# A gated delta rule inside a transformer trunk: queries and values turned by VectorE and DRAM instead of TensorE, log-gate sums spread by a repeating DMA read

## The chip, the cores and the metric

The kernel runs on one core of one Trainium2 chip. The metric is the device time of one launch in microseconds (us); the number compared is the median of several runs. A core has five engines that run their own instruction streams: TensorE (PE in the profile; its weight loads are listed apart as PEld), VectorE (DVE), ScalarE (ACT), GpSimd (POOL) and SyncE (SP), which in this kernel issues the DMAs. They meet by semaphores. Memory on the core is SBUF and the accumulators of TensorE, PSUM; DRAM is outside and reached by DMA.

## The reference

A trunk of two layers over a sequence of 1024 tokens with 1024 features, all in float32. Layer 0 mixes tokens by a gated spatial MLP beside a gated delta rule, layer 1 by differential attention; each layer then has an MLP and a gated projection. The change touches the delta rule of layer 0 only:

```python
def gated_deltanet(qkv, z, beta_logit, a_logit, conv_w, a_log, dt_bias, out_gain):
    qkv = silu(causal_depthwise_conv(qkv, conv_w))     # 4 taps
    q, k, v = split(qkv)                               # 4 heads of 128
    q = l2_normalize(q) * 128 ** -0.5
    k = l2_normalize(k)
    beta = sigmoid(beta_logit)
    g = -exp(a_log) * softplus(a_logit + dt_bias)      # log gates
    o = chunk_gated_delta_rule(q, k, v, g, beta)
    return rms_norm(o, out_gain) * silu(z)

def chunk_gated_delta_rule(q, k, v, g, beta):          # per chunk and head
    gc = cumsum(g)
    diff = gc[:, None] - gc[None, :]
    decay = where(causal, exp(diff), 0)
    a = where(strict, (k * beta) @ k.T * decay, 0)
    u = solve(a + I, v * beta)                         # unit lower triangular
    w = solve(a + I, k * beta * exp(gc)[:, None])
    qk = q @ k.T * decay
    # then, chunk after chunk, with a state S (128 x 128 per head):
    v_new = u - w @ S
    o = (q * exp(gc)[:, None]) @ S + qk @ v_new
    S = S * exp(gc[-1]) + (k * exp(gc[-1] - gc)[:, None]).T @ v_new
```

## The kernel before, in words

All large products are float32, made as three products of a high and a low part (`mm3`, L206), so most of TensorE's time goes to them, and ScalarE and VectorE split the operands into the parts (`split`, L222 to L224).

Activations lie with features on partitions and tokens along the free axis. The projection to queries, keys and values (`proj_qkv`) makes, per half of the sequence (512 tokens) and per 128 features, a PSUM tile of 128 x 512; VectorE adds the normalization's row factor, runs the four taps of the convolution, ScalarE a tanh, and VectorE finishes the silu into the home tile `qkv[i, hf]` (i is 0 for queries, 1 for keys, 2 for values; hf the half).

The delta rule works in 8 chunks (NC) of 128 tokens, 4 heads (G) each. It comes in four stages:

- `gates()`: TensorE makes the sums of log gates within each chunk, `gsum`, tokens on partitions, one column for each chunk and head.
- `ahead(c)`: for a chunk, the factors exp(gc_i - gc_j) as two masked tiles, `am` (strict) and `du` (causal, the other way round). One of the two sums must run along the free axis and be the same on all partitions; TensorE makes that spread: `pd` is gsum's column, broadcast, times an identity, in a high and a low part (`gparts`, `identr`). ScalarE takes the exponentials (L1602), GpSimd cuts the triangle (L1603). The keys are turned to tokens on partitions by TensorE (`pk`), normalized, and multiplied with themselves (`pkk`); VectorE puts the product and the mask together (L1628). Results go to DRAM (`spill`, and the diagonal blocks to `diag`).
- `solve()`: VectorE inverts the 32 x 32 diagonal blocks of all chunks at once, between filler work.
- the chunk loop: `inverse(c)` assembles the inverse of a chunk (`py`, `pz`), `prep(c)` turns the chunk's values and queries to tokens on partitions by TensorE transposes (`pv`, `pq`), scales the values (ScalarE), takes the queries' lengths and makes `pkq`; `step(c, state)` runs the recurrence (`pks`, `pvn`, `po`, `pst`). `prep(c + 1)` and `inverse(c + 1)` are issued beside `step(c)`.

Beside this chain of small matmuls runs a stream of filler units: the remaining projections, the spatial MLP's and the output's mm3 products, in pieces of a few large matmuls. `pump(n)` issues units up to a count; the numbers FILLA (40), FILLB (64), FILLC (48) and FILLS say how many units go beside each stage, and `share` deals them out over a stage's slots. The work of the chain is issued with priority; TensorE's own order follows the order in which the code asks for it, with a lag of 3 slots for filler. The other engines' queues are ordered by the scheduler of the framework from that program order. A PSUM buffer of the kind "aux" has two copies, shared by `pd` and `pkk`; a small pool of 4 SBUF tiles (`tmp`) serves tanh, convolution and others. SBUF tiles of fixed places (`slot`) are reused by name: "c2" and "c3" hold `du` of even and odd chunks, "c6" and "d0" hold `am`.

The last MLP of the kernel already has a turn through DRAM (L516 to L524): VectorE transposes a 128 x 512 tile in blocks of 32 x 32, and four DMAs, issued by SP, write its 32-row bands in runs of 32 numbers (128 bytes) to a DRAM tile `by_token`, so that a plain read returns the transposed tile.

## Time and profile before

| | us |
|---|---|
| median of 3 runs | 2506.88 (2506.01 to 2507.93) |
| the profiled execution | 2511.96 |
| its span | 2510.2 |
| TensorE busy | 2482.4 (99%) |
| VectorE busy | 1858.0 (74%) |
| ScalarE busy | 1288.9 (51%) |
| GpSimd busy | 315.3 (13%) |

The profile is one execution; its granted TensorE clock is 0.998 of full speed throughout. Busy is the time in which an engine worked, so a share of 99% means an engine with hardly any idle time, while an engine at 74% may still be full in one stage and idle in another. A row like "PE pkk L76 <- ACT dec L1602: 2.4, 2, 1.2" is a wait: the engine, its tile and line, then the engine and line that ended the wait, then us in total, how many times, and the longest. "x8" after a name counts instructions; a tile's name has no number where a view groups them. "landing" is the time from a DMA's issue until its data are there. Rows of a tile give the shortest, median and longest duration in ns, then the first and last start in us.

The layer-0 mixing covers the span's first 460 us: projections alone up to 95, `ahead` from 95 to about 145, `solve` to about 190, then the chunk loop.

### The profile page before, as it was taken

Reading aid. Unit: us, or ns where it says so; the run is one execution under the profiler, and the core shown is the slowest. Engines: PE = TensorE matmul, PEld = TensorE weight load, DVE = VectorE, ACT = ScalarE, POOL = GpSimd, SP = SyncE. Lnnn points to the kernel's source line nnn. Section 1 sums busy time; section 2 is a strip of 40 time slices with the busy share of each in tenths; the row PEclk is TensorE's granted clock in tenths of the full one; section 3 lists DMA queues with packets and bytes.
Section 4 is the critical chain, followed back from the end, with each engine's and each line's share of the span. In section 5 each row is a group of like instructions: output and inputs, shape, how many; then the busy total and the mean of one; then the engine's idle time right before and its main releaser. Section 6 shows DMA issues by size and latency. Waiting matters only on the chain.

```text
span 2510.2 us, 39961 instructions
## 1 busy us (share of the span) xinstructions
PE 2482.4 (99%) x13694; PEld 2117.7 (84%) x13694; DVE 1858.0 (74%) x3604; ACT 1288.9 (51%) x2585; POOL 315.3 (13%) x280
## 2 busy tenths in 40 slices
PE   9999999999999999999999999999999999999999
PEld 7898898888888887888899999987788888878877
DVE  7876767697667879566568888785886677888678
ACT  6543344465455444453356766664654445445443
POOL 0211232000000000000234443431000000000000
PEclk9999999999999999999999999999999999999999
DMA  7453435447556856653347776799475558657873
GB/s 237 128 161 84 134 111 180 145 157 239 173 195 208 271 178 196 188 172 115 118 96 170 164 170 152 168 250 279 127 229 194 178 189 275 214 189 202 232 221 109
DMA packets 530628, 451.46 MB, mean 180 GB/s; under 512 B 222484, under 2 KB 395512, under 8 KB 530424
## 3 DMA queue, kind: packets, MB, share of 16 engines
q1 hardware_dynamic: 530408, 448.90, 59.5%
q8 instruction: 108, 1.77, 0.3%
q14 instruction: 96, 0.79, 0.1%
q10 hardware_dynamic: 16, 0.00, 0.0%
HBM read 316.66 MB, written 132.12 MB: 179 GB/s over the span
## 4 chain that ended last, share of the span: by engine, by line
PE 92%; DMA 3%; DVE 3%; issue 1%; SPq 0%; ACT 0%; POOL 0%; DVEq 0%; ACTq 0%; POOLq 0%
PE mm L76 81%; PE po L76 3%; PE qk L76 3%; PE aux L76 2%; DMA raw<-in_w_ple_gate_dram 1%; PE tr L79 1%; DMA aT<-a_dram 1%; DVE w L224 0%; PE pz L76 0%; PE py L76 0%; PE aux L79 0%; PE pvn L76 0%; DMA ol<-o_dram 0%; PE pab L79 0%; PE pkq L76 0%
## 5 line engine op out<-in xcount | busy, mean ns | idle before, releaser
L76 PE MATMUL mm<-g,w 128*128 128x512 f32 x2592 | 603.8, 394 | 1.4 <-DVE acc L284 0.8
L223 ACT CAST w<-raw 128x512 fp32r<-128x512 f32 x598 | 365.6, 617 | 447.1 <-PE mm L76 348.5
L76 PEld LDWEIGHTS mm<-g,w 128*128 128x128 f32 x2592 | 485.8, 188 | 117.0 <-ACT w L223 1.2
L76 PE MATMUL mm<-hi,w 128*128 128x512 f32 x1728 | 554.3, 397 | 0.3 <-ACT hi L1268 0.3
L76 PE MATMUL mm<-w,hi 128*128 128x256 f32 (+2 forms) x2528 | 501.7, 294 | 1.3 <-ACT hi L223 1.3
L224 DVE TENSOR_TENSOR w<-raw,w 128x512 fp32r<-128x512 f32 x510 | 347.9, 690 | 169.1 <-ACT w L223 164.5
L76 PEld LDWEIGHTS mm<-w,hi 128*128 128x128 f32 x2528 | 400.8, 188 | 16.5 <-ACT hi L223 1.8
L76 PEld LDWEIGHTS mm<-hi,w 128*128 128x128 f32 x1728 | 324.9, 188 | 73.9 <-ACT hi L1268 0.7
L76 PE MATMUL mm<-w,lo 128*128 128x256 f32 (+2 forms) x1264 | 369.1, 293 | 0.8 <-DVE lo L224 0.8
L76 PE MATMUL mm<-lo,w 128*128 128x512 f32 x864 | 341.7, 396 | 0.9 <-DVE lo L1269 0.9
L76 PE MATMUL mm<-t,w 128*128 128x512 f32 x1152 | 270.8, 394 | 1.2 <-ACT w L223 1.2
L76 PEld LDWEIGHTS mm<-t,w 128*128 128x128 f32 x1152 | 216.2, 188 | 52.7 <-ACT w L223 1.6
L76 PEld LDWEIGHTS mm<-w,lo 128*128 128x128 f32 x1264 | 238.1, 188 | 7.1 <-DVE lo L224 1.2
L76 PEld LDWEIGHTS mm<-lo,w 128*128 128x128 f32 x864 | 162.8, 189 | 36.9 <-DVE lo L1269 1.4
L224 DVE TENSOR_TENSOR g<-graw,g 128x512 fp32r<-128x512 f32 x216 | 147.1, 685 | 12.7 <-DMA gd<-g 8.0
L223 ACT CAST g<-graw 128x512 fp32r<-128x512 f32 x216 | 132.7, 617 | 38.2 <-DMA graw<-gd 17.9
L260 POOL TENSOR_TENSOR r<-ms,mhalf 128x4 f32<-128x4 f32 x12 | 13.4, 1114 | 1043.0 <-DVE ms L258 1014.6
L1050 ACT ACTIVATE lg<-lg,nm 128x128 f32<-128x128 f32 (+7 forms) x128 | 99.2, 775 | 75.6 <-DVE nm L1047 74.7
L224 POOL TENSOR_TENSOR w<-raw,w 128x512 fp32r<-128x512 f32 (+1 forms) x88 | 114.9, 1325 | 145.9 <-ACT w L223 93.2
L350 ACT ACTIVATE g<-g 128x512 f32<-128x512 f32 x96 | 60.5, 631 | 116.5 <-DVE g L284 109.5
L1047 DVE CUSTOM_DVE_ANT_0 lg<-qk,al 128x512 f32<-128x512 f32 (+3 forms) x128 | 74.7, 587 | 28.9 <-PE qk L76 24.4
L76 PE MATMUL mm<-ohi,w 128*128 128x512 f32 x256 | 87.8, 408 | 0.0
(334 smaller groups left out, 3546.2 us busy)
## 6 DMA issues: line engine op xcount, KB each, us to landing
raw<-in_w_mlp_dram SPq DMA_DIRECT2D x352, 256.0 KB, 3.5
graw<-gd SPq DMA_DIRECT2D x224, 256.0 KB, 2.9
gd<-g SPq DMA_DIRECT2D x192, 256.0 KB, 3.3
raw<-in_w_ple_gate_dram SPq DMA_DIRECT2D x76, 256.0 KB, 3.3
acc<-h_dram SPq DMA_DIRECT2D x64, 256.0 KB, 4.3
keep<-in_w_mlp_dram SPq DMA_DIRECT2D x64, 256.0 KB, 4.2
raw<-in_w_in_e_dram SPq DMA_DIRECT2D x60, 256.0 KB, 3.5
h_dram<-acc SPq DMA_DIRECT2D x48, 256.0 KB, 2.6
```

The source lines that it names most:

```text
L76: self._next(self.engine.matmul(*a, **k))
L79: self._next(self.engine.transpose(*a, **k))
L223: self.nc.scalar.copy(hi, src)
L224: (lo_engine or self.nc.vector).tensor_tensor(lo, src, f32(hi), ALU.subtract)
L260: nc.gpsimd.tensor_tensor(r, ms, self.mhalf[:, 0:4], ALU.pow)
L350: nc.scalar.activation(g, src, AF.Relu)
L1047: nc.vector.tensor_tensor_reduce(out=lg[:, k0:k1], in0=ps[:, : k1 - k0], in1=al[:, u0 + k0 : u0 + k1], scale=-1.0, scalar=3.0e38 if c == 0 ...
L1050: nc.scalar.activation(lg[:, :n], lg[:, :n], AF.Exp, bias=nm[:, r, nch - 1 : nch], scale=-1.0, accum_out=me.sums[:, b, r : r + 1])
```

## The change

1. **The spread of the sums.** `ahead` loses its eight `pd` matmuls per chunk, and `gparts` and `identr` go. Instead `gates()` transposes `gsum` once on TensorE (`pgt`, 32 x 128), VectorE copies it, and SP writes it to a DRAM tile `g_dram`. `ahead(c)` begins with a DMA that reads the chunk's four rows (2 KB) into all 128 partitions of `du` (256 KB), yields, and takes both exponentials from that tile, the second in place.
2. **The interleaving of `ahead`.** A chunk's `ahead` has now three parts, and the loop over slots runs up to three chunks at once, with 10 slots for the 40 filler units instead of 9.
3. **Queries and values.** When a 128 x 512 tile of queries or values is ready, `turn()` transposes it in blocks on VectorE, and GpSimd issues four DMAs (64 KB each, runs of 128 bytes) to a DRAM tile `by_token`. There are 16 such tiles, so 16 transposes and 64 DMAs. `prep(c)` loses the TensorE transposes `pv` and `pq`; SP reads the chunk's values and queries, 256 KB each, from DRAM. ScalarE's scaling and squares then read SBUF instead of PSUM. Values have no home tile before that read.
4. **Smaller moves.** The spatial weights (`wsr`) are loaded early, into a place of their own, before the rest of the rows of x. The filler counts change: 108 units before `ahead` instead of 104, and 23 instead of 24 in each of the first four chunks. Keys are still turned by TensorE.

```diff
-FILLS = (24, 24, 24, 24, 28, 28, 28, 28)
+FILLS = (23, 23, 23, 23, 28, 28, 28, 28)
...
-        self.identr = self.cp.tile([P, P], F32R, name="identr")
-        nc.vector.tensor_copy(self.identr, self.ident)
...
         gsum, nsum = carve([P, NC, G], 0), carve([P, NC, G], 0)
-        gparts = self.cp.tile([P, 2, NC, G], F32R, name="gparts")
+        g_dram = self.dp.tile([NC * G, P], F32, name="g_dram")
...
             nc.vector.tensor_copy(flat(gsum), pg[:, 0])
-            self.split(flat(gsum), flat(gparts[:, 0]), flat(gparts[:, 1]))
+            pt = aux([NC * G, P], "aux", "pgt")
+            self.pe.transpose(pt, flat(gsum), self.ident)
+            gt = self.tmp(P)[0 : NC * G]
+            nc.vector.tensor_copy(gt, pt)
+            nc.sync.dma_start(g_dram, gt)
             nc.vector.tensor_scalar(flat(nsum), pg[:, 0], -1.0, None, ALU.mult)
-            wsr = self.tmp().rearrange("p (g t) -> p g t", g=G)
-            nc.sync.dma_start(wsr, ws.rearrange("g t s -> t g s"))
...
-        qkv, made = {}, set()
+        qkv, made, by_token = {}, set(), {}
+        def home(i, hf):
+            if (i, hf) not in qkv:
+                qkv[i, hf] = self.slot(f"A{i + 3 * hf}", [P, G, HT], F32, "qkv")
+        def turn(i, hf, m, y, t):
+            nc.vector.transpose(t, y)
+            for a in range(4):
+                f0 = m * P + 32 * a
+                nc.gpsimd.dma_start(by_token[i, hf].rearrange("(t c) f -> c t f", c=32)[:, :, f0 : f0 + 32], t[32 * a : 32 * a + 32].rearrange("c (t r) -> c t r", r=32))
+        def read_tokens(i, c, out):
+            hf, n = c // 4, c % 4
+            assert all((i, hf, m) in made for m in range(G))
+            nc.sync.dma_start(flat(out), by_token[i, hf][n * P : (n + 1) * P])
         def proj_qkv(i, j, hfs):
             def units(w):
                 for hf in hfs:
-                    if (i, hf) not in qkv:
-                        qkv[i, hf] = self.slot(f"A{i + 3 * hf}", [P, G, HT], F32, "qkv")
+                    if i != 2:
+                        home(i, hf)
+                    if i != 1 and (i, hf) not in by_token:
+                        by_token[i, hf] = self.dp.tile([4 * P, G * HD], F32, name=self.nm("by_token"))
...
                         th = self.tmp()
                         nc.scalar.activation(th, y, AF.Tanh, scale=0.5)
-                        nc.vector.scalar_tensor_tensor(qkv[i, hf][:, m % 4], th, 1.0, y, ALU.add, ALU.mult)
+                        z = y if i == 2 else qkv[i, hf][:, m % 4]
+                        nc.vector.scalar_tensor_tensor(z, th, 1.0, y, ALU.add, ALU.mult)
+                        if i != 1:
+                            turn(i, hf, m % 4, z, th)
...
         def ahead(c):
-            out = []
-            pd = aux([P, G, P], "aux", "pd")
-            for h in range(G):
-                for i in range(2):
-                    self.pe.matmul(pd[:, h], lhsT=gparts[:, i, c, h : h + 1].to_broadcast([P, P]), rhs=self.identr, start=i == 0, stop=i == 1)
-            for own, other in ((gsum, 1), (nsum, -1)):
-                e = self.slot(("c6", "d0")[c % 2] if other > 0 else f"c{2 + c % 2}", [P, G, P], F32, "dec")
+            du = self.slot(f"c{2 + c % 2}", [P, G, P], F32, "dec")
+            nc.sync.dma_start(flat(du), g_dram[G * c : G * c + G].rearrange("h t -> (h t)").partition_broadcast(P))
+            yield
+            am = self.slot(("c6", "d0")[c % 2], [P, G, P], F32, "dec")
+            for e, own, other in ((am, gsum, 1), (du, nsum, -1)):
                 for h in range(G):
-                    nc.scalar.activation(e[:, h], pd[:, h], AF.Exp, scale=-float(other), bias=own[:, c, h : h + 1])
+                    nc.scalar.activation(e[:, h], du[:, h], AF.Exp, scale=-float(other), bias=own[:, c, h : h + 1])
                 nc.gpsimd.affine_select(e, e, pattern=[[0, G], [-other, P]], base=0, channel_multiplier=other, compare_op=ALU.is_gt if other > 0 else ALU.is_ge, fill=0.0)
-                out.append(e)
-            am, du = out
             keep(c, 1, du)
...
         def prep(c):
-            k, v = part(1, c), part(2, c)
             kt = fetch(c, 2, self.slot(f"c{c % 2}", [P, G, HD], F32, "kt"))
             du = fetch(c, 1, self.slot(f"c{2 + c % 2}", [P, G, P], F32, "dec"))
-            pt = aux([P, G, P], "tr", "pv")
+            home(2, c // 4)
+            k, vb = part(1, c), flat(qkv[2, c // 4])[:, (c % 4) * HT : (c % 4 + 1) * HT].rearrange("p (h d) -> p h d", h=G)
+            read_tokens(2, c, vb)
+            if c == 0:
+                yield
+            q = part(0, c)
+            qt = self.slot(("d0", "c6")[c % 2], [P, G, HD], F32, "qt")
+            read_tokens(0, c, qt)
+            yield
             for h in range(G):
-                self.pe.transpose(pt[:, h], v[:, h], self.ident)
-            vb = v
-            for h in range(G):
-                nc.scalar.activation(vb[:, h], pt[:, h], AF.Copy, scale=hb[:, c, h : h + 1])
-            yield
-            q = part(0, c)
-            pt = aux([P, G, P], "tr", "pq")
-            for h in range(G):
-                self.pe.transpose(pt[:, h], q[:, h], self.ident)
-            rq = inverse_length(pt, "rq", self.slot(("d0", "c6")[c % 2], [P, G, HD], F32, "sq"))
+                nc.scalar.activation(vb[:, h], vb[:, h], AF.Copy, scale=hb[:, c, h : h + 1])
+            rq = inverse_length(qt, "rq", qt)
             yield
...
+        wsr = self.slot("c8", [P, G, P], F32, "wsr")
+        nc.sync.dma_start(wsr, ws.rearrange("g t s -> t g s"))
...
-        pump(104)
+        pump(108)
...
         systems = [ahead(c) for c in range(NC)]
-        for i, n in enumerate(share(FILLA, NC + 1)):
-            if i < NC:
-                run(systems[i], False)
-            if i:
-                run(systems[i - 1], False)
+        for i, n in enumerate(share(FILLA, NC + 2)):
+            for j in range(min(i, NC - 1), max(0, i - 2) - 1, -1):
+                run(systems[j], False)
             self.pe.slot()
             pump(done + n)
...
         f0 = prep(0)
-        chunk(none, invs[0], f0, FILLC, ("pi", "i", "i", "i", ""))
+        chunk(none, invs[0], f0, FILLC, ("pi", "i", "i", "i", "p"))
         chunk(none, none, f0, 0, ("p", "p"))
```

On TensorE, in the `ahead` stage before the change: the `pd` matmuls of a later chunk (`gparts` is the sums, `identr` the identity) come right ahead of the `pkk` (keys times keys) of an earlier one, and these ahead of transposes `pk`.

```order
L76 MATMUL mm_1324<-hi_201,w_1245 128x512
L76 MATMUL mm_1423<-hi_129,w_1080 128x512
L76 MATMUL mm_1423<-lo_130,w_1080 128x512
L76 MATMUL mm_1423<-hi_129,w_1081 128x512
L76 MATMUL pd_1268<-identr,gparts 128x128 x8
L76 MATMUL pkk_1310<-qkv_276 128x128 x4
L76 MATMUL mm_1423<-hi_138,w_1080 128x512
L79 MATMUL pk_1455<-ident,qkv_691 128x128 x3
L79 MATMUL pk_1526<-ident,qkv_691 128x128 x3
L76 MATMUL mm_1423<-lo_139,w_1080 128x512
```

And the same stage after the change:

```order
L76 MATMUL mm_1506<-hi_359,w_1091 128x512
L76 MATMUL mm_1506<-lo_360,w_1091 128x512
L76 MATMUL mm_1506<-hi_359,w_1092 128x512
L76 MATMUL mm_1506<-hi_405,w_1109 128x512
L76 MATMUL pkk_1414<-qkv_274 128x128 x4
L76 MATMUL pkk_1491<-qkv_274 128x128 x4
L79 MATMUL pk_1471<-ident,qkv_701 128x128
L79 MATMUL pk_1539<-ident,qkv_701 128x128
```

The `pd` rows are gone, and the `pkk` of two chunks follow each other.

GpSimd, in the `ahead` stage before: powers (`rk`), the masks (AFFINE_SELECT on `dec`, the tiles of `am` and `du`) and memsets.

```order
L1582 TENSOR_TENSOR rk_1465<-l_279_1462,mhalf 128x4
L1582 TENSOR_TENSOR rk_1536<-l_289_1533,mhalf 128x4
L1603 AFFINE_SELECT dec_1355<-dec_1355 128x512
L1603 AFFINE_SELECT dec_1361<-dec_1361 128x512
L1695 MEMSET xt_2338 128x512
L1695 MEMSET xt_2695 128x512
L1582 TENSOR_TENSOR rk_1624<-l_307_1621,mhalf 128x4
L1582 TENSOR_TENSOR rk_1695<-l_317_1692,mhalf 128x4
L1603 AFFINE_SELECT dec_1442<-dec_1442 128x512
L1603 AFFINE_SELECT dec_1448<-dec_1448 128x512
L1603 AFFINE_SELECT dec_1513<-dec_1513 128x512
L1603 AFFINE_SELECT dec_1519<-dec_1519 128x512
```

GpSimd in the same stage after, where `dec_1527`, `dec_1603` and `dec_1668` are `am` of chunks 5, 6 and 7:

```order
L1712 MEMSET xt_2326 128x512
L1379 DMA by_token_426<-t_1449 32x16x32 x4
L1623 AFFINE_SELECT dec_1527<-dec_1527 128x512
L1712 MEMSET xt_2718 128x512
L1604 TENSOR_TENSOR rk_1625<-l_306_1622,mhalf 128x4
L1623 AFFINE_SELECT dec_1457<-dec_1457 128x512
L1604 TENSOR_TENSOR rk_1690<-l_318_1687,mhalf 128x4
L1379 DMA by_token_1505<-t_1593 32x16x32 x4
L1623 AFFINE_SELECT dec_1603<-dec_1603 128x512
L1623 AFFINE_SELECT dec_1525<-dec_1525 128x512
L1379 DMA by_token_1505<-t_1734 32x16x32 x4
L1623 AFFINE_SELECT dec_1668<-dec_1668 128x512
```

Three groups of four DMAs of turned tiles stand in these rows between the masks; each waits for the VectorE transpose of its tile, and what is behind it in GpSimd's queue waits with it.

VectorE, in the `ahead` stage after: 21 rows stand between the filler weight `w_1656` (L222) and the operations that join product and mask of chunk 4 (`dec_1459` at L1646). These are the last of them, right behind the turn of a tile of values, STREAM_TRANSPOSE at L1376 (`carved` is a tile of small vectors):

```order
L222 TENSOR_TENSOR w_1836<-raw_1833,w_1835 128x512
L1636 TENSOR_SCALAR sc_1554<-rk_1549 128x4
L1639 TENSOR_TENSOR carved_240<-carved_240,rk_1549 128x4
L1420 TENSOR_SCALAR t_1588<-cx_1585,cols,t_1588 128x512
L1601 TENSOR_REDUCE l_318_1687<-sq_1685 128x4
L1632 TENSOR_TENSOR kt_1692<-pk_1680,carved_240 128x512
L1637 TENSOR_TENSOR sc_1486<-sc_1486,carved_240 128x4
L1602 TENSOR_SCALAR l_306_1622<-l_306_1622 128x4
L1637 TENSOR_TENSOR sc_1554<-sc_1554,carved_240 128x4
L1420 TENSOR_SCALAR t_1588<-cx_1585,cols,t_1588 128x512
L1602 TENSOR_SCALAR l_318_1687<-l_318_1687 128x4
L1646 TENSOR_SCALAR dec_1459<-pkk_1559,sc_1486,dec_1459 128x128 x4
```

TensorE uses that weight in the three rows ahead of the `pkk` of chunk 6, whose PSUM buffer these L1646 operations free:

```order
L76 MATMUL mm_1756<-w_1655,hi_199 128x256
L76 MATMUL mm_1756<-w_1656,hi_199 128x256
L76 MATMUL mm_1756<-w_1655,lo_200 128x256
L76 MATMUL pkk_1700<-qkv_701 128x128 x4
L76 MATMUL mm_1756<-w_1223,hi_127 128x256
```

Before the change, the rows around the same operations of VectorE (`dec_1442` and `dec_1513` are chunks 4 and 5) were these:

```order
L1404 TENSOR_SCALAR qkv_426<-t_1575,t_1570 128x512
L1628 TENSOR_SCALAR dec_1442<-pkk_1546,sc_1470,dec_1442 128x128 x4
L1395 TENSOR_TENSOR cx_1722<-mm_1579,rb_668 128x512
L1618 TENSOR_SCALAR sc_1700<-rk_1695 128x4
L1619 TENSOR_TENSOR sc_1700<-sc_1700,carved_242 128x4
L1620 TENSOR_TENSOR carved_242<-sc_1700,carved_242 128x4
L224 TENSOR_TENSOR w_1586<-raw_1583,w_1585 128x512
L1401 TENSOR_SCALAR t_1725<-cx_1722,cols,t_1725 128x512
L1628 TENSOR_SCALAR dec_1513<-pkk_1634,sc_1541,dec_1513 128x128 x4
```

Ahead of chunk 4's joining stand more rows than before: a turn, and the lengths, products and powers of the next chunks' keys (L1601, L1632, L1636, L1639).

VectorE at the start of the chunk loop, after the change (`qkv_2293` is queries; `inv_2317` the inverse of chunk 0, whose transpose TensorE's `py` waits for):

```order
L1424 TENSOR_SCALAR qkv_2293<-t_2376,t_2371 128x512
L1416 COPY carved_240<-cx_2437 128x3
L1420 TENSOR_SCALAR t_2441<-cx_2437,cols,t_2441 128x512
L1376 STREAM_TRANSPOSE t_2376<-qkv_2293 128x512
L1420 TENSOR_SCALAR t_2441<-cx_2437,cols,t_2441 128x512 x2
L1413 MEMSET cx_2539 128x3
L1758 TENSOR_SCALAR qkv_2336<-pks_2724,carved_240,qkv_2336 128x128 x4
L1424 TENSOR_SCALAR qkv_2293<-t_2446,t_2441 128x512
L1376 STREAM_TRANSPOSE t_2446<-qkv_2293 128x512
L1710 STREAM_TRANSPOSE inv_2317<-inv_2317 128x128
L1715 COPY xt_2326<-inv_2317 32x4x32 x4
```

Two turns of queries stand ahead of the transpose of `inv`; before, there were no turns on VectorE in this part.

## The prediction

> **What bounds the kernel now.** I read the busy totals first, then the chain of work that ended last, then the waits of the busiest engine in the stage that the change touches.
>
> ```profile
> span 2510.2 us, 39961 instructions
> PE 2482.4 (99%) x13694; PEld 2117.7 (84%) x13694; DVE 1858.0 (74%) x3604; ACT 1288.9 (51%) x2585; POOL 315.3 (13%) x280
> PE 92%; DMA 3%; DVE 3%; issue 1%; SPq 0%; ACT 0%; POOL 0%; DVEq 0%; ACTq 0%; POOLq 0%
> ```
>
> TensorE is busy 99% of the span and makes 92% of the chain. The change lies in the first 460 us (the even layer's mixing), so the question is whether TensorE is the limit there too. The windows answer that. Columns: length, then busy time of PE, PEld, DVE, ACT, POOL, each with its instructions; granted clock; DMA share; GB/s.
>
> ```profile
> 0.00:20.00 20.00, 16.86 (x73) 14.07 (x74) 11.33 (x24) 13.94 (x32) 0.69 (x6) 1.00 0.92 315
> 95.00:150.00 55.00, 52.61 (x347) 47.14 (x347) 48.48 (x127) 35.84 (x98) 19.02 (x24) 1.00 0.56 174
> 150.00:200.00 50.00, 50.00 (x387) 47.36 (x386) 31.93 (x85) 14.83 (x31) 0.20 (x1) 1.00 0.48 144
> 200.00:300.00 100.00, 100.00 (x806) 88.03 (x805) 70.23 (x167) 40.49 (x87) 20.31 (x23) 1.00 0.35 100
> 300.00:400.00 100.00, 99.03 (x939) 93.39 (x938) 74.56 (x186) 44.05 (x105) 39.51 (x34) 1.00 0.39 123
> ```
>
> 95 to 150 us is the preparation of the eight chunks (`ahead`), 150 to 190 the small solves, the rest the chunk loop. TensorE has no slack after 150; before it, it idles 2.4 of 55 us, and VectorE is at 48.5 of 55: the one stage where a second engine is close. What those 2.4 us are:
>
> ```profile
> PE pkk L76 <- ACT dec L1602: 2.4, 2, 1.2
> PE pkq L76 <- DVE state L1760: 0.5, 1, 0.5
> PE po L76 <- DVE dec L1676: 0.4, 1, 0.4
> ```
>
> The matmuls `pkk` (keys by keys) twice waited for the exponentials that read `pd`, whose PSUM buffers they share. All other waits of the chunk loop are 0.5 us or less.
>
> **The change, part by part.** Matmuls removed: 64 `pd` (the spread of log gates), 32 `pv` and 32 `pq` (transposes of values and queries); one transpose `pgt` is added. Their own durations overlap, so I take what they occupy in the chain:
>
> ```profile
> 139.48 0.84 PE pd L76 x8
> 140.32 0.94 PE pkk L76 x8
> 218.42 0.44 PE pv L79 x4
> ```
>
> 0.84/8 = 0.105 us per `pd`, 0.44/4 = 0.11 per `pv`; `pq` has the same shape as `pv`. 64 x 0.105 + 64 x 0.11 = 13.8, less 0.1 for `pgt`: **-13.7 us**, all on the bound engine. Filler matmuls keep their number; the shift of four units (23 for 24, 108 for 104) only moves them.
>
> The exponentials now read an SBUF tile that a DMA fills, so `pkk` no longer queues for `pd`'s buffers: **-2.4 us**, if nothing else is late. What is late next is the rest of this part.
>
> *VectorE in the preparation.* Four of the sixteen new stream transposes fall there. The last MLP already turns tiles in this way, which gives the price:
>
> ```profile
> L521 DVE STREAM_TRANSPOSE t<-acc x16: 702/704/715, 2266.7 to 2414.7; 128x512 f32<-128x512 f32 x16
> 115.46 0.68 DVE L1579 TENSOR_REDUCE l<-sq 128x4 f32<-128x512 f32 x1
> 116.06 0.68 DVE L1614 TENSOR_TENSOR kt<-pk,carved 128x512 f32<-128x512 f32 x1
> 118.65 0.16 DVE L1392 COPY cx<-carved 128x3 f32<-128x3 f32 x1
> ```
>
> In the order above, 21 VectorE rows now stand between the filler weight that TensorE uses just before the `pkk` of chunk 6 and the four operations that free the buffer for that `pkk` (those on chunk 4's `dec`). Twelve of them are 512 wide, at 0.60 between starts (0.70 for the transpose), some 7.6 us; nine small ones at about 0.17 make 1.5: 9.1 us. If that weight comes just in time, TensorE waits 9 us; if VectorE runs ahead of it, 0. No wait of TensorE on such a weight is among the rows above, but the engine is 88% busy and gets 2.8 us more; I take the middle, **+4.5** (0 to 9).
>
> *VectorE at chunk 0.* Two turns, 1.4 us, and the convolution rows between them stand ahead of the transpose of `inv` for which `py` waits; half of four: **+2** (0 to 4). The other ten transposes, 7 us, run beside TensorE in stages where VectorE is 64 to 75% busy: nothing; without that cover they cost the 7.
>
> *GpSimd.* It issued no DMA before; now it issues 64, and 16 of them stand in the preparation between its masks and powers. The trace has no such issue. The same transfer issued by SP, and its landing:
>
> ```profile
> L524 SPq DMA_DIRECT2D by_token<-t x64: 303/488/2018, 2267.4 to 2418.4; - x64
> by_token<-t SPq DMA_DIRECT2D x64, 64.0 KB, 2.9
> L1582 POOL TENSOR_TENSOR rk<-l,mhalf 128x4 f32<-128x4 f32 x6 | 6.9, 1168 | 1.3 <-DVE l L1580 1.3
> L1603 POOL TENSOR_SCALAR_AFFINE_SELECT dec<-dec 128x512 f32<-128x512 f32 x16 | 11.2, 707 | 28.8 <-ACT dec L1602 24.9 <-DMA raw<-in_w_in_e_dram 3.1 <-POOL dec L1603 0.8
> ```
>
> The bounds are 0.49 (median on SP) and 2.0 (the longest there). I take 1.0, the geometric middle, which also lies at GpSimd's own floor here: a power of 128x4 elements takes 1.17. Then GpSimd is busy 19 + 16 = 35 of some 45 us; a mask that stands behind a group of four comes up to 4 us later than before, and I put **+1** on the path. [...]
>
> *DMA.* Every round trip is a load that must be early enough.
>
> ```profile
> dec<-spill SPq DMA_DIRECT2D x8, 256.0 KB, 3.0
> acc<-by_token SPq DMA_DIRECT2D x12, 256.0 KB, 3.5
> 130.36 2.12 DMA spill<-dec
> L1602 ACT ACTIVATE dec<-pd,carved x64: 352/395/501, 105.1 to 143.9; 128x128 f32<-128x128 f32 x64
> ```
>
> The repeating read of the sums (256 KB written, 2 KB source) should land like `dec<-spill`, 3.0 us; it is issued a stage before its exponentials, and three stages of the preparation are now interleaved, not two. It needs a buffer that is freed by the previous write to `spill` (2.1 us), as before. Each of the two buffers serves four chunks, and one round of it is 9.7 us: read 3.0, eight exponentials 3.2 (0.395 each), two masks 1.4 (0.707 each), write 2.1. Four rounds make 39 us, which fit the stage of about 45: nothing, and beyond that it is what the buffer is short of. Values and queries come back in 16 reads of 3.5 us, one stage ahead of their use: nothing; on SP they wait for the GpSimd writes, and the `diag`, `spill` and sum rows queue behind them. The spatial weights' load moves ahead into 0.92 DMA share: 256 KB at 315 GB/s is 0.8 us at most, taken as 0. For all small new exposures of the chunk loop together **+1** (0 to 5).
>
> Sum: -13.7 - 2.4 + 4.5 + 2 + 1 + 1 = -7.6. The profiled execution took 2511.96, 1.8 above its span and 5.1 above the median of the runs, so 2504.4 for such an execution and 2499.3, say **2499**, against the median of 2506.88.
>
> **The rivals.** *GpSimd's queue becomes the bound of the preparation (slower).* Its 19 us of work there plus 16 issues pass 45 us at (45 - 19)/16 = 1.6 us each, and earlier where groups of four stand ahead of a mask: half way, 1.3. At 2.5 us it needs 59 us, 14 more than there are, and the last mask stands behind a group of 10 us, of which I count half: +19. The other terms without GpSimd's own +1 make -8.6, so +10.4, **2517**. For it: a DMA here is 512 runs of 128 bytes, the longest issue on SP took 2.0, and a mask that is late delays all of its chunk. Against it: the median of 0.49, and 24.9 us in which GpSimd stood waiting for exponentials and could have issued. Chance 0.26.
>
> *The pile on VectorE eats the gain (same).* With both VectorE terms at their ends, 9 + 4, the sum is -13.7 - 2.4 + 13 + 2 = -1.1: **2505.8**. For it: 48.5 of 55 us busy before; against it: no wait on a filler weight. Chance 0.13.
>
> *The DMA engines become the bound of the preparation (slower).* There, eight reads of 256 KB, 16 writes of 64 KB in short runs and four reads of values add 4.2 MB to the 9.6 that 174 GB/s makes in 55 us: 251 GB/s, against the 315 at a share of 0.92. If landings double, a buffer's round is 9.7 + 5.1 = 14.8 us, four rounds 59 us in place of 39: +20, with the rest at -7.6 **2519**. Against it: 0.56 of the DMA engines was used. Chance 0.10.
>
> *The short runs take far longer than beside a calm queue (slower).* If a write of `by_token` took eight times the 2.9 us of its row, 23 us, SP would stand 20 us longer at the first read of values, with `diag` behind it: -7.6 + 20, **2519**. The row itself, for the same shape, speaks against it, so 0.04. [...]
>
> **How the numbers follow.** My forecast has 0.47. A change of this kernel's time below 0.2%, 5 us, can't be told from none. Faster 0.47; same 0.13; slower 0.26 + 0.10 + 0.04 = 0.40. The range reaches from 2490 (no new wait at all: 2506.9 - 16.1 = 2490.8) to 2523, a little above the slow rivals, since a GpSimd issue over 2.5 us isn't excluded. Inside its own case the forecast lies at 2490 to 2502.
>
> **What would show it.** Right: no rows of `pd`, `pv`, `pq`; TensorE's idle time in 95 to 150 us near 5, before `pkk`, ended by VectorE's `dec`; GpSimd's DMA issues near 1 us; no wait of SP on `by_token` over 3 us. GpSimd's rival: issues over 1.6 us, masks waiting behind them, TensorE waiting for `pkk` with GpSimd's `dec` at the end of the chain. DMA's rival: landings of `spill` and the sums over 5 us. The forecast fails above all if a GpSimd issue costs more than the 1 us that I gave it, for nothing in the trace shows one.

## The result

The changed kernel takes 2514.8 us (median of 7 runs, 2507.6 to 2520.2) against 2506.0 beside it: a ratio of 1.0035, 95% interval 1.0025 to 1.0046, so 9 us slower where 7.6 faster were forecast. Ratios, here and below, leave out the one execution that stands far off (3543.6 us, of the kernel `sp_issue`). The two profiled executions don't show this in their totals: that of before was the slowest of its runs (2511.96), that of after one of the faster (2512.24). They are compared here by stage, up to the first matmul of layer 0's MLP that reads the tile `g` (rows of the tile view: engine, operation, count, shortest/median/longest ns, first and last start in us); before first, then after:

```profile
L76 PE MATMUL mm<-g,w x2592: 387/394/499, 815.2 to 2400.0; 128*128 128x512 f32 x200
```

```profile
L76 PE MATMUL mm<-g,w x2592: 387/394/497, 821.1 to 2400.7; 128*128 128x512 f32 x200
```

5.9 us are lost by then, although 13.7 us of matmuls are gone: some 20 us were lost in the mixing.

The page of after, with the chain that ended last, and its windows (columns as before):

```profile
span 2510.5 us, 39916 instructions
PE 2471.1 (98%) x13567; PEld 2105.3 (84%) x13567; DVE 1869.3 (74%) x3619; ACT 1292.1 (51%) x2586; POOL 355.6 (14%) x344
PE 88%; DVE 4%; DMA 4%; issue 2%; SPq 1%; ACT 1%; POOL 0%; DVEq 0%; ACTq 0%; POOLq 0%
```

```profile
95.00:150.00 55.00, 45.68 (x272) 40.37 (x271) 45.09 (x120) 30.47 (x81) 24.72 (x33) 0.94 0.68 194
150.00:200.00 50.00, 49.37 (x368) 46.80 (x368) 29.51 (x81) 24.71 (x57) 4.50 (x7) 1.00 0.58 182
200.00:300.00 100.00, 95.27 (x749) 82.43 (x748) 76.95 (x174) 36.35 (x73) 38.29 (x51) 0.97 0.48 131
300.00:400.00 100.00, 96.59 (x858) 90.62 (x857) 77.70 (x183) 43.43 (x102) 47.47 (x47) 0.98 0.54 166
```

TensorE now idles 9.3 us in the preparation (2.4 before), 4.7 at 200 to 300 and 3.4 at 300 to 400 (0 and 1.0 before), and of these four windows the granted clock is under 1.00 in just these three. (In the first 20 us it is 0.91 where it was 1.00; several of the kernels below have that, the fastest among them.) Its waits in the mixing:

```profile
PE pkk L76 <- DVE dec L1646: 8.6, 1, 8.6
PE po L76 <- DVE qkv L1758: 2.6, 1, 2.6
PE mm L76 <- DVE alo L1574: 2.2, 1, 2.2
PE py L76 <- issue: 1.8, 1, 1.8
```

The first, on TensorE's timeline and on VectorE's:

```profile
132.31 0.28 PE L76 MATMUL mm<-w,lo 128*128 128x256 f32 x1
141.21 2.08 PE L76 MATMUL pkk<-qkv 128*128 128x128 f32 x8 [8.63 <-DVE dec L1646]
142.94 0.78 PE L76 MATMUL mm<-w,hi 128*128 128x256 f32 x2
```

```profile
130.93 0.75 DVE L222 TENSOR_TENSOR w<-raw,w 128x512 fp32r<-128x512 f32 x1 [0.62 <-ACT w L221]
135.91 0.69 DVE L1376 STREAM_TRANSPOSE t<-t 128x512 f32<-128x512 f32 x1
140.04 1.11 DVE L1646 SCALAR_TENSOR_TENSOR dec<-pkk,sc,dec 128x128 f32<-128x128 f32 x4
```

From the filler weight (130.93) to the joining of chunk 4 (140.04) VectorE works through the heap of rows: 9.1 us. After the wait eight matmuls take 2.08 us; eight such matmuls of the kernel before take 1.11.

What leads the stage is in the chain of the window 95 to 150 us, by line; before, then after:

```profile
by line: PE mm L76 33.4%; DVE dec L1628 7.6%; issue 6.1%; ACT dec L1602 5.6%; PE pkk L76 5.4%; SPq L1631 5.2%; DVE l L1579 4.3%; DMA spill<-kt 4.0%; DMA spill<-dec 3.9%; PE pd L76 3.2%; DVE sc L1618 3.0%; POOL rk L1582 2.6%; DVE kt L1614 2.
```

```profile
by line: DMA spill<-dec 34.9%; ACT dec L1622 11.1%; PE mm L76 9.7%; DMA spill<-kt 9.2%; DMA dec<-g_dram 7.7%; issue 5.2%; SPq L1649 4.5%; SPq L1617 2.5%; DMA g_dram<-t 2.5%; ACT t L1422 1.8%; SPq L1608 1.6%; PE pk L79 1.6%; DVE t L1424 1.4%
```

The preparation was led by TensorE's filler, and is now led by DMA, 54% of the chain (spill writes, the reads and the write of the sums). The landings in that window, after (us last; x is the count), and SP's wait at L1617, where it issues the reads of the sums:

```profile
spill<-dec SPq DMA_DIRECT2D x12, 256.0 KB, 3.6
dec<-g_dram SPq DMA_DIRECT2D x8, 256.0 KB, 4.3
by_token<-t POOLq DMA_DIRECT2D x12, 64.0 KB, 3.9
SPq L1617 <- DMA spill<-dec: 3.3, 6, 1.0
```

Two buffers take turns, so the first two reads find theirs free; each of the other six waited on SP for the write that empties its buffer. And what came of the exponentials (their row before, in the prediction, runs from 105.1 to 143.9) and to the start of the small solves, which read `diag` when all chunks are done; the solves' row of before stands first, the other two are of after:

```profile
L1640 SPq DMA_DIRECT2D work<-diag x2: 320/375/430, 151.7 to 152.1; - x2
```

```profile
L1622 ACT ACTIVATE dec<-dec,carved x64: 384/387/403, 107.3 to 159.1; 128x128 f32<-128x128 f32 x64
L1658 SPq DMA_DIRECT2D work<-diag x2: 320/372/424, 168.3 to 168.7; - x2
```

From the first exponential to the last it is 51.8 us where it was 38.8, and the solves start 16.6 us later. Before, they ended with a write at 183.1 and the first `py` came at 195.9, 12.8 us later. Not all of that is slack: now the write is at 203.3 and `py` at 211.9, 8.6 us behind it, and in the kernel whose `py` waits longest (`fill48`, below) it is 7.2 (219.1 and 226.3). So at most 5.6 us were to spare. They are used up, and TensorE waits 1.8 us for `py` at chunk 0.

### The profile page after: what moved, and what is told of

It reads as the page before. It is cut to its first block, busy times and chain, and to the rows that moved or that the text cites. A ratio compares the mean times of both kernels' runs of the same rounds, so it can differ in the third digit from the quotient of the medians.

```text
span 2510.5 us, 39916 instructions
## 1 busy us (share of the span) xinstructions
PE 2471.1 (98%) x13567; PEld 2105.3 (84%) x13567; DVE 1869.3 (74%) x3619; ACT 1292.1 (51%) x2586; POOL 355.6 (14%) x344
## 4 chain that ended last, share of the span: by engine, by line
PE 88%; DVE 4%; DMA 4%; issue 2%; SPq 1%; ACT 1%; POOL 0%; DVEq 0%; ACTq 0%; POOLq 0%
PE mm L76 77%; PE po L76 3%; PE qk L76 3%; PE aux L76 2%; DMA spill<-dec 1%; PE tr L79 1%; DVE w L222 1%; DMA raw<-in_w_mlp_dram 0%; DMA guv<-uv_dram 0%; ACT dec L1622 0%; DMA aT<-a_dram 0%; DMA raw<-in_w_ple_gate_dram 0%; PE pvn L76 0%; PE aux L79 0%; PE py L76 0%
## 5 line engine op out<-in xcount | busy, mean ns | idle before, releaser
L222 DVE TENSOR_TENSOR w<-raw,w 128x512 fp32r<-128x512 f32 x510 | 349.5, 693 | 174.5 <-ACT w L221 166.7
L222 DVE TENSOR_TENSOR g<-graw,g 128x512 fp32r<-128x512 f32 x216 | 147.2, 685 | 11.0 <-DMA gd<-g 7.4
L222 POOL TENSOR_TENSOR w<-raw,w 128x512 fp32r<-128x512 f32 (+1 forms) x88 | 115.0, 1326 | 142.8 <-ACT w L221 75.9
```

The costliest lines, as they stand in the source:

```text
L222: (lo_engine or self.nc.vector).tensor_tensor(lo, src, f32(hi), ALU.subtract)
```

## The experiments

Times are medians; ratios are to the kernel before, beside each, with 95% intervals. "Solves" is the start of `work<-diag` in the run's profile.

| kernel | us | ratio | solves at |
|---|---|---|---|
| neither part, new filler counts | 2505.9 | 1.0001 (0.9992 to 1.0009) | 152.4 |
| queries turned | 2502.0 | 0.9981 (0.9972 to 0.9990) | 151.5 |
| values turned | 2510.8 | 1.0017 (1.0009 to 1.0026) | 153.5 |
| the same again | 2510.9 | 1.0011 (1.0002 to 1.0020) | 155.5 |
| both turned | 2506.9 | 1.0005 (0.9997 to 1.0014) | 154.3 |
| spread alone | 2514.1 | 1.0037 (1.0024 to 1.0050) | 161.7 |
| all (the change) | 2514.8 | 1.0035 (1.0025 to 1.0046) | 168.3 |

**The parts.** My theories: V, VectorE's heap, lengthened by the turns; D, the DMA round trip of the sums. Each kernel restores one part of the code before. The three-part interleaving goes with the spread: `spread_only` has it, `turn_only` not, and no run separates the two.

```diff
 # spread_only: turns undone
-                        if i != 1:
-                            turn(i, hf, m % 4, z, th)
 # turn_only: ahead() and its loop as before, in two parts, with pd
```

> The sums of log gates spread by the DMA read, with the three-part preparation and the new filler counts as in the changed kernel; queries and values are turned by TensorE as before. Theory V (the 8.6 us wait of pkk is VectorE's pile, which the turns lengthen; the turns also delay chunk 0): the pkk wait shrinks to 0-3 us, no wait at chunk 0, so the 64 pd and the old 2.4 us wait are won: 2506 - 9 = about 2497 to 2500. Theory D (the DMA read of the sums and its buffer's round trip make masks and powers late): the pkk wait stays at 6-9 us and the clock falls behind it: 2505 to 2509.

> Queries and values turned by VectorE and DRAM, with the new filler counts; the sums spread by TensorE as before, with the two-part preparation. Theory V: a pkk wait of 4-9 us remains, with waits of 4-5 us and a slow clock at chunk 0, against 7.1 us of pv and pq won: 2508 to 2513. Theory D: no pkk wait above the old 2.4 us; chunk 0 alone is lost: 2504 to 2507.

> Only the new filler counts and the early load of the spatial weights; the rest as before. Both theories: as the kernel before within 2 us (2504 to 2508). If it is slower by 4 us or more, the moved filler is itself a cause.

The spread alone is as slow as the whole change. V had 2497 to 2500 for it and fell; D had 2505 to 2509, the right side but too small, and its own sign, a `pkk` wait of 6 to 9 us, failed too. TensorE waits elsewhere, all on VectorE, and the clock of 95 to 150 us is 0.91:

```profile
PE mm L76 <- DVE w L222: 4.8, 2, 4.2
PE pv L79 <- DVE kt L1627: 4.4, 1, 4.4
PE pkk L76 <- DVE dec L1641: 2.1, 1, 2.1
```

Both turned came out at 2506.9, in D's range (2504 to 2507), but with a `pkk` wait of 3.6 us, where D had 2.4 at most. The new filler counts alone change nothing, as both theories said. Within their intervals the parts add up: values and queries -0.5 us together by their own ratios (+4.3 and -4.8), +1.3 measured for both at once; with the spread's +9.3 that makes 10.6, and 8.8 was measured. Against their matmuls: queries give 4.8 (3.5 expected), values lose 4.3 where 3.5 were to be won, the spread loses 9.3 where 6.7 and the old wait were to be won.

```diff
-                nc.gpsimd.dma_start(by_token[i, hf]...
+                nc.sync.dma_start(by_token[i, hf]...
```

> The changed kernel, with the 64 DMAs of the turned tiles issued by SP instead of GpSimd. Rival G of the prediction (GpSimd's queue is the bound): 8 us faster than the changed kernel, 2506 or less. Theories V and D: GpSimd's 0.65 us per issue is not what TensorE waits for, so no gain; SP takes 64 x 0.49 us more and stands at each turn: 2513 to 2520.

2511.7, ratio 1.0019 (1.0011 to 1.0028), with the `pkk` wait at 8.7 us as in the change: GpSimd's queue is not the main cause, since the rival built on it had 2506 or less. SP as issuer is some 3 us better by the medians, with intervals that just overlap; V and D had it no better (2513 to 2520).

```diff
 # queries_only: the turn for i == 0 alone
-                        if i != 1:
+                        if i == 0:
                             turn(i, hf, m % 4, z, th)
 # values_only, values_again: i == 2 alone
```

> Of the turns only the queries' eight; values are turned by TensorE and the sums spread by TensorE as before; new filler counts. Turning both gave 2506.9 where 2498.8 (2505.9 less 7.1) was to be expected. If the values' turns, which lie in the preparation, lose it (pkk wait 3.6 us and the clock): 2502 to 2503. If the queries' turns lose it: 2506 to 2508.

> Of the turns only the values' eight; queries turned and sums spread by TensorE as before. If the values' turns alone lose what turn_only lacks (a pkk wait of 3.6 us and the clock behind it): 2505.9 - 3.5 + 5 = 2506 to 2509. If it takes both kinds of turns together: 2501 to 2504.

> The kernel with the values' turns alone once more, for a second profile: its first one (2505.3) was the fastest of its executions (up to 2516). If executions differ by waits in the preparation, this profile shows a pkk wait over 4 us in 95 to 150 us at a time over 2509; if by something outside the mixing, the first 460 us are alike.

The queries' turns lie at the start of the chunk loop and in it (in the changed kernel turns from 205 to 294 us, reads from 235 to 392), where most tiles are written well before they are read: faster than the kernel before, as expected. Of the values' eight turns four lie in the preparation or right behind it (123 to 152 us in the changed kernel), and turning the values loses more than the 2506 to 2509 expected. Their second profile (2510.9) shows the wait expected, which the first, at 2505.3, had at 1.8 us; the rows are a wait of TensorE and, behind it, one of ScalarE in 95 to 160 us:

```profile
PE pkk L76 <- ACT dec L1622: 4.1, 1, 4.1
ACT dec L1622 <- DMA spill<-dec: 4.4, 1, 4.4
```

Spill writes land in 3.2 us there (2.2 before). The exponentials wait for a buffer that is still being written to DRAM; in the kernel before they did so too, but in three waits of 3.9 us together.

Over all kernels below, those whose solves start at 161.7 or later took 2511 us or more, while 157.9, 158.7 and 160.3 still went with 2507.7, 2504.8 and 2503.6. That goes together, one profile for each kernel; it is not shown as the cause. Only three of the late kernels have a wait of TensorE for `py` (the change, and the two with more cover below); the others lose their time earlier, and the values alone took 2511 with the solves at 153.5 and 155.5.

**Cover, and reads without a buffer's round trip.**

```diff
 # early: all eight reads at once, into places free until the values need them
+        spread = [self.slot(t, [P, 4, G, P], F32, "spread") for t in ("A2", "A5")]
+        for c in range(NC):
+            nc.sync.dma_start(flat(spread[c // 4][:, c % 4]), g_dram[...].partition_broadcast(P))
-                    nc.scalar.activation(e[:, h], du[:, h], AF.Exp, ...
+                    nc.scalar.activation(e[:, h], src[:, h], AF.Exp, ...
 # fill48, and early_fill with both edits
-FILLA, FILLB, FILLC = 40, 64, 48
+FILLA, FILLB, FILLC = 48, 56, 48
 # early and early_fill: also two parts per chunk again, and 9 slots (left out here)
```

> The changed kernel, but the repeating reads of all eight chunks go to tiles of their own (256 KB each, in the place that the values use later) right after the sums are written, so no read waits for a buffer that must first be written to DRAM; the preparation is again in two parts per chunk. Turns as in the changed kernel. Theory D (the buffer's round trip makes the masks late): the 8.6 us wait and the slow clock behind it go; against turn_only (2506.9) the 64 pd (6.7 us) and its 3.6 us pkk wait are won: 2496 to 2501. Theory V (VectorE's pile): 2512 to 2516, as the changed kernel.

> The changed kernel with 48 filler units beside the preparation instead of 40, and 56 instead of 64 beside the small solves: about 10 us more cover. If TensorE only comes too early to a chain that takes its fixed time (theories D and V alike), the 8.6 us wait and the 2 us of slow clock go and nothing comes back at the solves, which end 14 us before they are needed: 2503 to 2506. If the solve then is late at chunk 0: 2510 or more.

> Both edits: early reads and 48/56 filler units. Theory D: like the early reads alone or 1-2 us better, 2495 to 2500. Theory V: like the filler alone, 2503 to 2506.

Early reads missed, alone and with more cover (D had 2496 to 2501 and 2495 to 2500); more cover alone came out by the second of its cases, 2510 or more with late solves. Early reads: 2511.7, 1.0021 (1.0012 to 1.0030), some 3 us of the 9, with the `pkk` wait still 9.9; more cover: 2529.6, 1.0090 (1.0076 to 1.0103); both: 2517.0, 1.0040 (1.0027 to 1.0054). With more cover the `pkk` wait falls, but the solves start at 175.8, and the time comes back at chunk 0:

```profile
PE py L76 <- issue: 10.9, 1, 10.9
PE mm L76 <- ACT t L1493: 9.7, 3, 5.3
PE pkk L76 <- DVE dec L1646: 3.1, 1, 3.1
```

My reading is that more filler beside the chain gives ScalarE and VectorE, which serve both, more to do, and that less is left beside the solves; no run separates the two.

**Order or round trip.** In the order of VectorE, the key work of chunks 4 to 7 (eight wide rows) stands in one heap of 30 rows ahead of chunk 4's joining in the changed kernel, in two portions of four before. Theory O takes this for the cause. One test takes the reads away (the factors are then all 1: this part of the computation is left out), another gives the order back by a 4-column matmul per chunk in `pd`'s PSUM place.

```diff
 # no_spread: no reads, and two parts per chunk as before the change
+ nc.scalar.activation(e[:, h], gsum[:, c, h : h + 1].to_broadcast([P, P]), AF.Exp, ...
 # anchor
+            pd = aux([P, G, P], "aux", "pd")
+            self.pe.matmul(pd[:, 0, 0:4], lhsT=self.ident, rhs=gsum[:, c], start=True, stop=True)
+            nc.scalar.copy(an, pd[:, 0, 0:4])
 # no_spread_anchor: both edits, two parts per chunk
```

> The changed kernel without any spread of the sums: the exponentials read the chunk's own column of sums instead (all factors become 1, so this part of the computation is left out); no repeating reads, two parts per chunk. Theory D (the DMA round trip): with no read to wait for, the pkk wait and the slow clock go: 2506.9 less 6.7 less some 5, 2495 to 2500. Theory O (order: without the pd matmuls the key work of four chunks stands in one heap ahead of chunk 4's joining on VectorE, 38 rows here): a pkk wait of 6 to 10 us stays, 2505 to 2513.

> The changed kernel with one 4-column matmul per chunk into a PSUM buffer of the kind that pd had, which ScalarE copies and uses as the bias; nothing else. It costs TensorE under 1 us in all and restores the old rhythm of the order: the key work stands in two portions of four rows. Theory O: the 8.6 us wait falls below 4 us: 2502 to 2508. Theory D: the reads and their buffers are unchanged: 2513 to 2517.

> The kernel without any spread (all factors 1, this part of the computation left out), now with the small matmul per chunk that restores the rhythm of the order: the key work ahead of chunk 4's joining falls from eight rows to four. With the anchor alone (2517) and without the reads alone (2504.8) this completes the square. If order and DMA trip each cost something of their own: the 7.9 us wait shrinks to under 3 us and the time falls to 2496 to 2500. If the order costs nothing (the anchor only adds its own waits): 2504 to 2508.

Without reads 2504.8, 0.9993 (0.9984 to 1.0001): 10 us less than the change, though the wait is there as O said; D had 2495 to 2500. With the order restored and the reads kept 2517.0, 1.0041 (1.0028 to 1.0053). With both 2506.9, 0.9999 (0.9990 to 1.0008), the heap's wait gone. `pkk`'s waits, without reads, and then with both edits, where `pd` is the small matmul and `an` its copy:

```profile
PE pkk L76 <- DVE dec L1644: 7.9, 1, 7.9
```

```profile
PE pd L76 <- DVE dec L1648: 1.3, 1, 1.3
PE pkk L76 <- ACT an L1620: 0.7, 2, 0.4
```

So the reads, with the third part that came with them, cost 10 us in either order (2514.8 to 2504.8, 2517.0 to 2506.9). How they cost it is less plain. Without them the exponentials run from 95.3 to 146.6 us: 51.3 us, as long as in the change, but starting 12 us earlier, since they wait neither for the sums' write nor for a read. So this test takes away the late start and the buffers' rounds at once.

The order shows no cost in the medians, but that doesn't clear it. The small matmul has a price: in the next section it makes a kernel whose longest wait is 2.4 us slower by 7.0. If it costs the same here, the wait of 7.9 us cost some 5, an estimate (7.0 less the 2.0 between 2504.8 and 2506.9). There is room for it: without the reads the change's 13.7 us of matmuls are gone as well, and only 2 are won, so some 12 are still lost, about 8 of them with the values' turns if the parts add up. The longest wait of the trace, the one that I had located, is then a part of the loss, and not the larger one.

**A faster kernel.**

> Queries turned by VectorE and DRAM, values by TensorE, sums spread by the repeating read, with the small matmul per chunk that keeps the order. Theory O: 2502.0 (queries alone) less 6.7 for 64 pd and plus 1 for the small ones: 2495 to 2500, faster than both kernels. Theory D: a pkk wait of 6 us or more: 2505 to 2512.

> Queries turned by VectorE and DRAM, values by TensorE; the sums spread by repeating reads that all start at once into the places that the queries use later, so that no read waits for a buffer. No small matmul. If the buffer's round trip is what the spread loses: 2502.0 less 6.7, 2495 to 2499. If the order (eight key rows in two portions here, 20 rows ahead of chunk 4) still makes TensorE wait 5 us or more: 2500 to 2505.

> The same with the small matmul per chunk. If it only adds waits of its own (2.5 to 3.7 us of pkk on its copy in the two kernels that had it): 1 to 4 us slower than without. If it mends the order: 1 to 4 us faster.

Values stay on TensorE in all three. With the anchor 2502.4, 0.9981 (0.9972 to 0.9989), between the ranges of both theories. With early reads (into the places of the queries) and no anchor **2496.6, 0.9959 (0.9946 to 0.9973)**: 10 us faster than before, the 10.2 that its 96 matmuls were worth (64 `pd`, 32 `pq`), and in the range expected if the buffer's round trip is what the spread loses. It has two parts per chunk again, so that is not shown apart from the interleaving. Early reads with the anchor: 2503.6, 0.9984 (0.9975 to 0.9992), 7.0 us slower where 1 to 4, either way, were expected, with `pkk` waiting 4.2 us for the anchor's copy. The fastest kernel's solves and its largest wait behind the start:

```profile
L1656 SPq DMA_DIRECT2D work<-diag x2: 320/372/423, 154.0 to 154.3; - x2
PE pkk L76 <- DVE dec L1644: 2.4, 1, 2.4
```

The queries with the spread as in the change, no early reads and no anchor, were not run; by adding the parts they would be at 2511, so that early reads are worth some 14 us there is argued, not shown.

**Load or wait.**

```diff
 # dead_writes: values turned and written, and TensorE turns them as well
 # dead_reads: the eight repeating reads into free places; pd as before, nothing reads them
+        dead = [self.slot(t, [P, 4, G, P], F32, "dead") for t in ("A0", "A3")]
```

> Values are turned by VectorE and written by GpSimd's DMAs as in the changed kernel, but nothing reads them: TensorE turns the values as before, and queries and sums are as before. The extra work is 8 transposes on VectorE, 32 GpSimd DMAs and 2 MB of writes. If these alone (VectorE's place, or the load of the short runs on the DMA engines) slow the preparation: 5 to 8 us over the kernel before, 2511 to 2515, with spill writes landing in 2.8 us or more. If the reads of the values or their place on SP do it: 2505 to 2508.

> The sums are also written to DRAM, and the eight repeating reads of 256 KB start at once, but nothing uses them: TensorE spreads the sums as before, queries and values as before. If the load of 2 MB of repeating reads is what the spread loses: 2512 to 2518, with spill writes landing in 2.8 us or more. If it is the wait for a read and its buffer: 2505 to 2508.

2507.7, 1.0007 (0.9996 to 1.0017), and 2507.0, 1.0001 (0.9993 to 1.0010). The load as such costs nothing that can be told (at most 4.3 and 2.5 us, by the intervals), although spill writes land in 2.6 and 2.8 us with it. What remains is the work that waits for the data, by elimination. For the values that is the less certain, since the intervals of dead writes and of values turned overlap.

## Why the prediction was wrong

- *Matmuls, -13.7*: right as a price. Queries and spread together gave 10.3 us (6.8 to 13.5 by the interval) for matmuls priced at 10.2, once little waited.
- *The old wait, -2.4*: it went, and 8.6 came. It was also a reading of one execution, the slowest: with the new filler counts alone the profile has 0.7.
- *VectorE's heap, +4.5 (0 to 9)*: place and rows were right, and the wait took the upper end, 8.6. Not counted was the clock: the window of the stage has 0.94 for 1.00, and the eight matmuls behind the wait took 2.08 us. But as the whole cause it was wrong: spread alone, without turns, lost as much with a `pkk` wait of 2.1, and with the wait still at 7.9 the kernel without reads is 10 us faster. What the wait itself cost is open, some 5 us by the estimate above.
- *Chunk 0, +2 (0 to 4)*: 2.6 + 1.8 = 4.4, and a clock of 0.97 in that window. Two turns alone don't make it: both turned without the spread, solves at 154.3, shows no wait over 1 us there. So it goes with the late solves; that they are the cause is argued, since the `po` wait ends with VectorE's L1758, a little behind a turn.
- *GpSimd, +1*: an issue costs 0.66 us, not 1.0 (row below), and its rival of 26% fell. The 1.17 called GpSimd's floor is none: a mask took 0.71 in the kernel before (mean of 16). That its 2517 lies near the 2514.8 measured is chance.

```profile
L1379 POOL DMA_DIRECT2D by_token<-t x64 | 42.1, 663 | 65.3 <-DVE t L1376 60.1 <-DVE mean L1525 5.0
```

- *DMA, 0*: **the step that failed.** "Four rounds make 39 us, which fit the stage of about 45: nothing": the round was put at 9.7 us, with landings of 3.0 and 2.1 taken from the kernel before, where the stage had eight reads less, and with little margin. Measured instead: the reads and the third part that came with them cost 10 us. Landings are 4.3 and 3.6, a round is 4.3 + 3.1 + 1.3 + 3.6 = 12.3, four rounds 49, and the exponentials took 51.8. The third rival had this mechanism, at landings doubled (+20 for the stage; the solves came 16.6 later), and got 10%. Its reason, DMA engines as the bound, was only half right: load alone, without a reader, costs nothing that can be told. The sum of a round is not the whole account either. In spread alone it is 11.1, four 44, and the exponentials took 49.7; without the reads only 3.1 + 1.3 + 2.2 = 6.6 are left, four 26, and they took 51.3; with queries and anchor, reads and buffers as in the change, they took 42.7. How the 10 us divide between the later start (107.3 for 105.1), the rounds and the interleaving stays open.
- *The short runs, eight times 2.9 us (4%)*: no run shows the eight times; in the change the writes of `by_token` landed in 3.9 us in the preparation (median of 12).
- *Values' reads, 0*: wrong by 6 to 8 us for the values, right for the queries: the same operation, but one of them has half its turns in the stage whose chain is now made of DMA.

The time lies inside the range given, but through another case than the one forecast: the change makes the kernel slower.

## What to carry to other kernels

Before matmuls are replaced by a round trip through DRAM, look which chain will lead the stage then, not only which engine leads now: here 0.1 us matmuls went, and DMA came to lead the stage (54% of its chain), with a buffer that is filled and emptied by it. A round that fits a stage with little margin may not fit it once its own transfers slow the landings (the eight dead reads alone took those of the spill writes from 2.2 to 2.8 us; in the change they were 3.6). Try places of their own for such reads, all started at once, and do it where the data are wanted late: with the queries alone turned this made the fastest kernel here, with the values turned as well it won back some 3 us of 9. And don't take the longest wait of a trace for the whole loss: test it, with an edit whose own price is known.

## What was not expected of the hardware

- After an idle stretch of 8.6 us the next matmuls ran at about half speed for some 3 us (eight `pkk` 2.08 us against 1.11 in the kernel before), and the granted clock of 142 to 150 us was 0.84. The slow rows end at 144.4, 3.2 us after the wait. In shorter windows the granted clock is 1.00 up to 137.5 us, 4.9 us into the wait, 0.50 from 138 to 144, and 1.00 again from 144.5.
- GpSimd's issue of a 64 KB DMA in runs of 128 bytes takes 0.65 us, nearly the same each time (651 ns shortest and median, 855 longest), where SP's, in the last MLP of the kernel before, took from 0.30 to 2.0.
- DMA traffic that nothing waits for did not change the time by an amount that can be told. Eight dead reads of 256 KB raised the DMA share of the stage from 0.56 to 0.66 and the landings of the spill writes from 2.2 to 2.8 us (time 1.0001, 0.9993 to 1.0010). With the dead writes, twelve of 64 KB in the stage, it was 0.59 and 2.6 us (1.0007, 0.9996 to 1.0017).
